# A chunked RWKV-7 recurrence: products of 64 x 64 in quarters of the array in place of products over the whole array

## The chip, the cores and the metric

One core of a Trainium2 chip runs one launch. The metric is the device time of that launch in microseconds, median of three runs; the kernel before has 4324.55 us (4307.94 to 4329.31). All data of the part that is changed is float32.

## The reference, cut to what matters

Two blocks of a network follow each other. The second mixes 1280 tokens (256 of context, 1024 others) with three branches: a state-space branch, an RWKV-7 branch, and a gated linear attention. The change lies in the RWKV branch alone, which has 4 heads of 64 features, is run forward and backward, and is this scan:

```python
def step(S, inp):
    r_t, w_t, k_t, v_t, kk_t, a_t = inp
    sa = -jnp.einsum('nhvk,nhk->nhv', S, kk_t)
    S = S * w_t[:, :, None, :] + sa[..., None] * (kk_t * a_t)[:, :, None, :] + v_t[..., None] * k_t[:, :, None, :]
    return S, jnp.einsum('nhvk,nhk->nhv', S, r_t)
```

Outputs are wanted for the 1024 other tokens only; the context tokens feed the state.

## The kernel before, in words

`mixers` (L1350) runs the three branches. `rwkv_prep` has written, ahead of the loop, the scaled features of each stretch of 128 tokens (`rec`: b, c, p, and for the 1024 tokens q) and the inverses of small triangular blocks (`xd`) to memory. `rwkv_loop` (L1629) does the scan in chunks of 64 tokens (two to a stretch of 128, j = 0, 1), for two heads at a time (h = 0, 1). It has 40 items: 2 pairs of heads (ft) x 2 directions (d) x 10 stretches (g). Per item the steps are:

- `fetch`: loads `rec` and, at times, the inverses `XD`.
- `pairs` (L1671, per head): the masked products of features over tokens, `M`, 128 tokens x 128 tokens per head, of which the blocks off the chunks' diagonal are masked to zero.
- `rights` (L1683): three transposes by TensorE, a product with the values, and two copies by ScalarE: right sides `R`, and `bc`.
- `solve0`, `solve1`, `solve2`: multiply by the block inverse, by the off-diagonal block, and by the inverse again (ScalarE, VectorE, ScalarE copy out); they give `U`.
- `steps` (L1722, per chunk): the map of the state over one chunk, as a 128 x 128 block matrix `gt` of two heads, and what is added, `ze`. Only its diagonal 64 x 64 blocks are written (VectorE adds the identity at L1737, ScalarE scales at L1738); the rest stays zero from six tiles cleared once.
- `queries`, `inside`: the queries carried to the chunk's start, and the part of the output within the chunk.
- `states` (L1767, per chunk): the output from the state (`yp`) and the new state `S`, 128 x 128 with two diagonal blocks. This is the only chain from item to item.

The steps of several items overlap: `seq` (L1794) gives each step a lag in items and an order. `YP` says behind which steps the loop yields; at each yield `mixers` runs a part of the side work, 3 parts an item: `gla` (gated attention; its scores are L1971 on TensorE and L1976, a masked copy, on VectorE) and then `ssd`. Over the first items it also runs `gates`, vector products whose weights are loaded (L167). Within this order a scheduler places each engine's instructions by when it thinks their inputs come. Each engine then runs its list in order.

PSUM has eight banks. In the loop `LPS` gives four to the loop's steps (`mm`), two to side work (`tr`), one to `po` (the state's output) and one to the gates (`gv`):

```python
YP = 7, 12
LPS = dict(mm=4, tr=2, po=1, gv=1)
seq = ((fetch, 0), (rights, 3), (steps, 4, 0), (solve0, 3), (steps, 4, 1), (solve1, 3), (queries, 4),
       (states, 5, 0), (solve2, 3), (inside, 4), (pairs, 2, 0), (states, 5, 1), (pairs, 2, 1))
```

A float32 product is two instructions on TensorE (each with its load of the stationary operand); a transpose is one.

Of the kernel before, what the change touches and what calls it, by code (L numbers as in the profile page):

```python
# [20 lines left out]
P = 128  # L21
# [18 lines left out]
class K:  # L40
# [176 lines left out]
YP = 7, 12  # L217
LPS = dict(mm=4, tr=2, po=1, gv=1)
# [907 lines left out]
def b2_constants():  # L1126
# [3 lines left out]
    same = (s // 64) == (t // 64)  # L1130
    lo, hi = (s % 64) < 32, (t % 64) >= 32
# [8 lines left out]
    put("m_0", np.concatenate([same & lo & hi, same & (s <= t), same & (s < t), same & (s <= t)], 1))  # L1140
    put("m_1", np.concatenate([same & ~lo & ~hi, same & (s >= t), same & (s > t), same & (s >= t)], 1))
# [26 lines left out]
class Mixer:  # L1168
# [460 lines left out]
    def rwkv_loop(self, es):  # L1629
# [12 lines left out]
        mm = [self.const(sp, f"m_{d}").rearrange("p (m a b) -> p m a b", m=2, a=2) for d in range(2)]  # L1642
        NG = 6
# [3 lines left out]
        for t in xds + gts + zes:  # L1647
            nc.gpsimd.memset(t, 0.0)
        n_step, S, n_xd, xd_now = [0], [None], [0], {}

        def fetch(st, it):
            ft, d, g, first = it
            rec = sp.tile([P, 4, P], F32, name="rec", bufs=6)
            w_ = 4 if g >= CT else 3
            k.load(rec[:, :w_], self.rec_d[d][ft][g].rearrange("p (a n) -> p a n", n=P)[:, :w_])
            si = 0 if g < CT else 1 + (g - CT) // 4
            g0, ng = CHUNKS[si][0] // P, CHUNKS[si][1] // P
            if (ft, d, si) not in xd_now:
                xt = xds[n_xd[0] % 3]
                n_xd[0] += 1  # L1660
                src = self.xd[d][ft][si]
                for bb in range(4):
                    o = slice(bb * 32, bb * 32 + 32)
                    for h in range(2):
                        k.load(xt[o, h, :ng, o], src[h * ng:(h + 1) * ng, bb].rearrange("n s t -> s n t"))
                xd_now[ft, d, si] = xt
            st.update(b=rec[:, 0], c=rec[:, 1], p=rec[:, 2], pq=rec[:, 2:2 + w_ - 2],
                      X=xd_now[ft, d, si][:, :, g - g0], V=vtm[:, g, ft * P:(ft + 1) * P]
                      .rearrange("p (h x) -> p h x", x=64))

        def pairs(st, it, h):  # L1671
# [3 lines left out]
            if h == 0:  # L1675
                st["M"] = sp.tile([P, 2, 2, 2, P], F32, name="M", bufs=3)
            f = slice(64 * h, 64 * h + 64)
            pm = k.bank().rearrange("p (m a b) -> p m a b", m=2, a=2)[:, :, :w_]
            for m, src in ((0, st["b"]), (1, st["c"])):
                nc.tensor.matmul(pm[:, m], src[f], st["pq"][f], start=True, stop=True)  # L1680
            nc.vector.tensor_tensor(st["M"][:, h, :, :w_], pm, mm[d][:, :, :w_], op=OP.mult)

        def rights(st, it):  # L1683

            M, V = st["M"], st["V"]
            ps = k.bank()
            nc.tensor.transpose(ps[:, :P], st["p"], k.ident)
            for i, nm in enumerate("bc"):
                nc.tensor.transpose(ps[:, (2 + i) * P:(3 + i) * P], st[nm], k.ident)
            for h in range(2):  # L1690
                nc.tensor.matmul(ps[:, P + h * 64:P + h * 64 + 64], M[:, h, 1, 0], V[:, h], start=True, stop=True)
            R = sp.tile([P, 2, 2, 64], F32, name="R", bufs=2)
            nc.scalar.activation(R, ps[:, :2 * P].rearrange("p (a h x) -> p h a x", h=2, x=64), AF.Copy)
            bc = sp.tile([P, 2, P], F32, name="bc", bufs=2)
            nc.scalar.activation(bc, ps[:, 2 * P:].rearrange("p (a n) -> p a n", n=P), AF.Copy)
            st.update(R=R.rearrange("p h a x -> p h (a x)"), bt=bc[:, 0], ct=bc[:, 1])

        def solve0(st, it):
            U1 = sp.tile([P, 2, P], F32, name="U1", bufs=2)
            ps = k.bank()  # L1700
            for h in range(2):
                nc.tensor.matmul(ps[:, h * P:(h + 1) * P], st["X"][:, h], st["R"][:, h], start=True, stop=True)
            nc.scalar.activation(U1, ps[:, :2 * P].rearrange("p (h x) -> p h x", x=P), AF.Copy)
            st["U1"] = U1

        def solve1(st, it):
            ps = k.bank()
            U1 = st["U1"]
            for h in range(2):
                nc.tensor.matmul(ps[:, h * P:(h + 1) * P], st["M"][:, h, 0, 0], U1[:, h], start=True, stop=True)  # L1710
            nc.vector.scalar_tensor_tensor(U1, ps[:, :2 * P].rearrange("p (h x) -> p h x", x=P), -1.0, st["R"],
                                           op0=OP.mult, op1=OP.add)

        def solve2(st, it):
            U = sp.tile([P, 2, 2, 64], F32, name="U", bufs=2)
            ps = k.bank()
            for h in range(2):
                nc.tensor.matmul(ps[:, h * P:(h + 1) * P], st["X"][:, h], st["U1"][:, h], start=True, stop=True)
            nc.scalar.activation(U, ps[:, :2 * P].rearrange("p (h a x) -> p a h x", a=2, x=64), AF.Copy, scale=-1.0)
            st["U"] = U  # L1720

        def steps(st, it, j):  # L1722

            ft, d, g, first = it
            V, U = st["V"], st["U"]
            ch = slice(64 * j, 64 * j + 64)
            e = self.eend[:, ft, d, 2 * g + j:2 * g + j + 1]
            gt, ze = gts[n_step[0] % NG], zes[n_step[0] % NG]
            n_step[0] += 1
            ps = k.bank()  # L1730
            nc.tensor.matmul(ps[:, :P], U[ch, 0], st["bt"][ch], start=True, stop=True)
            pz = ps[:, P:2 * P].rearrange("p (h x) -> p h x", x=64)
            nc.tensor.matmul(pz, st["bt"][ch], U[ch, 1], start=True, stop=False)
            nc.tensor.matmul(pz, st["ct"][ch], V[ch], start=False, stop=True)
            for h in range(2):
                f = slice(64 * h, 64 * h + 64)
                nc.vector.tensor_tensor(gt[f, f], ps[f, f], k.ident[f, f], op=OP.add)  # L1737
                nc.scalar.activation(ze[f, f], ps[f, P + 64 * h:P + 64 * h + 64], AF.Copy, scale=e[f])  # L1738
            st["step", j] = gt, ze, e

        def queries(st, it):
            if it[2] < CT:
                return
            qt = sp.tile([P, P], F32, name="qt", bufs=2)
            ps = k.bank()
            for h in range(2):
                nc.tensor.matmul(ps[64 * h:64 * h + 64, :P], st["U"][:, 0, h], st["M"][:, h, 0, 1], start=True, stop=True)
            nc.vector.tensor_tensor(qt, ps[:, :P], st["pq"][:, 1], op=OP.add)
            st["qt"] = qt

        def inside(st, it):
# [5 lines left out]
            yc = k.bank()[:, :P].rearrange("p (h x) -> p h x", x=64)  # L1757
            for h in range(2):
                nc.tensor.matmul(yc[:, h], M[:, h, 1, 1], V[:, h], start=True, stop=False)
                nc.tensor.matmul(yc[:, h], M[:, h, 0, 1], U[:, 1, h], start=False, stop=True)  # L1760
            o = Y[:, g - CT, 2 * ft:2 * ft + 2]
            if d == 0:
                nc.scalar.activation(o, yc, AF.Copy)
            else:
                nc.vector.tensor_tensor(o, yc, o, op=OP.add)

        def states(st, it, i):  # L1767
            ft, d, g, first = it
            j = i if d == 0 else 1 - i
            if first and i == 0:  # L1770
                S[0] = sp.tile([P, P], F32, name="S", bufs=3)
                nc.gpsimd.memset(S[0], 0.0)
            ch = slice(64 * j, 64 * j + 64)
            gt, ze, e = st["step", j]
            if g >= CT:
                if i == 0:
                    st["yp"] = k.bank(tag="po")[:, :P].rearrange("p (h x) -> p h x", x=64)
                nc.tensor.matmul(st["yp"][ch], st["qt"][:, ch], S[0].rearrange("p (h x) -> p h x", x=64), start=True,
                                 stop=True)
            ps = k.bank()  # L1780
            nc.tensor.matmul(ps[:, :P], gt, S[0], start=True, stop=True)
            S[0] = sp.tile([P, P], F32, name="S", bufs=3)
            nc.vector.scalar_tensor_tensor(S[0], ps[:, :P], e, ze, op0=OP.mult, op1=OP.add)
            if g >= CT and i == 1:
                o = Y[:, g - CT, 2 * ft:2 * ft + 2]
                nc.vector.tensor_tensor(o, st["yp"], o, op=OP.add)
# [1135 lines left out]
```

## Time and profile before

| | |
|---|---|
| runs | 4324.55 us median (4307.94, 4324.55, 4329.31) |
| profiled execution | 4346.18 us, its span 4344.4 us |
| TensorE busy in the span | 3970.7 us (91%), 23047 products' instructions |
| VectorE | 2888.9 us (66%) |
| ScalarE | 1993.5 us (46%) |
| GpSimd | 1175.7 us (27%) |
| mean granted clock of TensorE | 0.94 |

The clock is a share of 2.4 GHz: 1.00 is 2.4 GHz, 0.50 is 1.2 GHz. Products are pipelined, so a row's duration of one product holds its way through the array; how fast they follow each other is read from the starts of a timeline. A busy share over the whole span is a mean over stages of different kinds; the loop is about an eighth of it.

### The profile page before, as it was taken

The page shows a single profiled execution, that of the slowest core. Times are in us where ns is not written, and L with a number is a line of the kernel's source. Part 1 is how long each engine was busy: PE and PEld are TensorE (multiplying, and loading weights), DVE is VectorE, ACT ScalarE, POOL GpSimd, SP SyncE. Part 2 cuts the span into 40 slices and gives each one's busy share as a digit, 9 for nine tenths or more (in the row PEclk, how much of TensorE's full clock was granted, in tenths as well). Part 3 has the DMA queues.
Part 4 walks back from the last instruction along what each step waited for, and adds up shares of the span by engine and source line. Part 5 has one row for each costly group of instructions (what it writes and reads, how often), then busy time and mean ns, then how long its engine had stood idle before and what let it go on. Part 6 is the DMA issues. An engine that isn't in the chain of part 4 may idle for free. (4 is left out here: it accounts for less than half of the span.)

```text
span 4344.4 us, 63290 instructions
## 1 busy us (share of the span) xinstructions
PE 3970.7 (91%) x23047; PEld 3033.1 (70%) x23048; DVE 2888.9 (66%) x5672; ACT 1993.5 (46%) x4292; POOL 1175.7 (27%) x1211
## 2 busy tenths in 40 slices
PE   6999899999998999999997999999999998999993
PEld 4787566667775666688786788777777666666662
DVE  4673577764745778645765655667778777776774
ACT  4122366653122666423353233433257666666664
POOL 1200133332101333321333531122313232233323
PEclk7999899999998999999997899799999999999996
DMA  5121600123123001344444511215368888889885
GB/s 152 34 66 40 166 13 13 31 81 109 43 63 107 8 13 35 113 120 129 126 124 130 143 35 34 74 42 185 118 210 293 286 247 272 267 261 274 261 264 163
DMA packets 371321, 558.89 MB, mean 129 GB/s; under 512 B 52126, under 2 KB 285056, under 8 KB 346048
## 3 DMA queue, kind: packets, MB, share of 16 engines
q1 hardware_dynamic: 335728, 432.81, 31.2%
q0 software_dynamic: 35280, 122.02, 11.0%
q8 instruction: 182, 2.98, 0.3%
q14 instruction: 131, 1.07, 0.1%
HBM read 438.42 MB, written 116.33 MB: 128 GB/s over the span
## 5 line engine op out<-in xcount | busy, mean ns | idle before, releaser
L98 DVE TENSOR_TENSOR wa_lo<-w_raw,wa_hi 128x512 fp32r<-128x512 f32 x520 | 340.4, 688 | 59.5 <-ACT wa_hi L97 56.7
L97 ACT ACTIVATE wa_hi<-w_raw 128x512 fp32r<-128x512 f32 x520 | 303.5, 625 | 99.3 <-PE mm L109 48.5
L107 PE MATMUL mm<-hh,w_hi 128*128 128x512 f32 (+1 forms) x848 | 320.7, 379 | 4.1 <-ACT h L266 3.3
L108 PE MATMUL mm<-hl,w_hi 128*128 128x512 f32 (+1 forms) x848 | 319.8, 377 | 0.3 <-DVE hl L269 0.3
L109 PE MATMUL mm<-hh,w_lo 128*128 128x512 f32 (+1 forms) x848 | 318.0, 375 | 0.0
L941 ACT ACTIVATE pe<-mm 128x512 f32<-128x512 f32 (+1 forms) x336 | 193.3, 588 | 153.4 <-PE mm L109 124.7
L907 DVE TENSOR_REDUCE mx<-mm 128x1 f32<-128x512 f32 (+1 forms) x400 | 224.3, 587 | 51.6 <-PE mm L906 49.3
L107 PE MATMUL mm<-wa_hi,xh 128*128 128x512 f32 (+3 forms) x632 | 257.6, 408 | 0.5 <-ACT xh L97 0.5
L108 PE MATMUL mm<-wa_lo,xh 128*128 128x512 f32 (+3 forms) x632 | 251.0, 397 | 1.2 <-DVE wa_lo L98 1.2
L109 PE MATMUL mm<-wa_hi,xl 128*128 128x512 f32 (+3 forms) x632 | 250.2, 396 | 0.0
L946 POOL TENSOR_TENSOR pl<-pe,ph 128x512 fp32r<-128x512 f32 x96 | 142.6, 1487 | 333.0 <-ACT ph L945 326.1
L2644 POOL DMA_INDIRECT acc_d<-y,ix x97 | 172.5, 1778 | 202.7 <-DMA acc_d<-y,ix 54.7
L946 DVE TENSOR_TENSOR pl<-pe,ph 128x512 fp32r<-128x512 f32 (+1 forms) x240 | 202.2, 855 | 36.9 <-ACT ph L945 35.8
L610 DVE SCALAR_TENSOR_TENSOR acc<-zc,b_v,acc 128x512 f32<-128x512 f32 (+1 forms) x300 | 199.3, 712 | 1.5
L2600 PE MATMUL mm<-ident,xg 128*128 128x128 f32 (+5 forms) x840 | 121.7, 291 | 85.0 <-DMA xg<-h_d,ix 84.8
L2589 POOL COPY wc<-xg 128x1 f32<-128x1 f32 (+5 forms) x97 | 47.8, 492 | 531.6 <-DMA xg<-h_d,ix 528.4
L107 PEld LDWEIGHTS mm<-hh,w_hi 128*128 128x128 f32 x848 | 162.0, 191 | 40.1 <-issue 7.4
L2600 PEld LDWEIGHTS mm<-ident,xg 128*128 128x128 f32 (+5 forms) x840 | 110.7, 199 | 112.6 <-issue 99.3
L107 PE MATMUL mm<-wb_hi,hidh 128*128 128x512 f32 (+5 forms) x420 | 186.8, 445 | 0.0
L108 PEld LDWEIGHTS mm<-hl,w_hi 128*128 128x128 f32 x848 | 162.1, 191 | 33.8 <-issue 6.5
L97 ACT ACTIVATE w_hi<-w_raw 128x1024 fp32r<-128x1024 f32 x61 | 64.6, 1060 | 259.5 <-PE mm L108 230.6
L109 PEld LDWEIGHTS mm<-hh,w_lo 128*128 128x128 f32 x848 | 162.2, 191 | 28.8 <-issue 1.3
(782 smaller groups left out, 11555.7 us busy)
## 6 DMA issues: line engine op xcount, KB each, us to landing
w_raw<-in_exp_w_dram SPq DMA_DIRECT2D x192, 1024.0 KB
w_raw<-in_w_in_dram SPq DMA_DIRECT2D x69, 512.0 KB
gemv_w<-in_w_mod_dram SPq DMA_DIRECT2D x48, 512.0 KB
gemv_w<-in_ada_w_dram SPq DMA_DIRECT2D x48, 512.0 KB
rec<-rec SPq DMA_DIRECT2D x64, 256.0 KB
wo_raw<-in_w_out_dram SPq DMA_DIRECT2D x20, 512.0 KB
y<-ydram SPq DMA_DIRECT2D x36, 256.0 KB
xt<-in_x_dram SPq DMA_DIRECT2D x16, 512.0 KB
```

Source lines behind the costliest of these rows:

```text
L97: nc.scalar.activation(hi, src, AF.Copy)
L98: eng.tensor_tensor(lo, src, f32(hi), op=OP.subtract)
L107: mm(out, ah, bh, start=start, stop=False)
L108: mm(out, ah, bl, start=False, stop=False)
L109: mm(out, al, bh, start=False, stop=stop)
L610: nc.vector.scalar_tensor_tensor(o, zc[:, ft, p0 + j:p0 + j + c[1]], v["cfw"][:, 2 * j + ft:2 * j + ft + 1], o, op0=OP.mult, op1=OP.add)
L907: nc.vector.tensor_reduce(mx[:, t, c:c + 1], ps[:, :n], axis=AX.X, op=OP.max)
L941: nc.scalar.activation(pe, ps, AF.Exp)
L946: (nc.gpsimd if j % PLP == PLP - 1 else nc.vector).tensor_tensor(pl, pe, f32(ph), op=OP.subtract)
L2589: nc.gpsimd.tensor_copy(st.wc[:n], st.x[:n, D + st.r:D + st.r + 1])
L2600: nc.tensor.transpose(ps[:, j * n:(j + 1) * n], xk[:, 4 * q + j], k.ident[:n, :n])
L2644: nc.gpsimd.indirect_dma_start(out=self.acc_d, out_offset=bass.IndirectOffsetOnAxis(ap=st.ix[:n, 0:1], axis=0), in_=y[:n], in_offset=None, ...
```

## The change

Every product of the loop becomes one of 64 rows (the contracted dimension) by 64 columns, in one of four quarters of the array; the four products of a step, one for each head h and chunk j, go to the four quarters. What a step writes goes to a pair of banks (`pair`), the bank chosen by which half of the rows the product reads. Layouts alternate: where a step reads partitions by heads it writes partitions by chunks, and the other way round. `M` holds only the 64 x 64 diagonal blocks, the state is 128 x 64 (two heads, no zero blocks), the identity is added by a product with the identity matrix in place of VectorE's sum, and the query's carry is part of `steps`. The transposes are plain products with the identity (`turn`). The state is copied out in halves by VectorE and ScalarE. Three pairs serve the loop, one bank side work, one the gates; the chain over items is six deep. Cut to its core:

```diff
+    def pair(self):
+        return self.ps.tile([P, 2, 512], F32, name="m2", tag="m2", bufs=self.bufs["m2"])
-YP = 7, 12
-LPS = dict(mm=4, tr=2, po=1, gv=1)
+YP = 5, 10
+LPS = dict(m2=3, tr=1, gv=1)
...
-        gts = [sp.tile([P, P], F32, name=f"gt{i}") for i in range(NG)]
-        zes = [sp.tile([P, P], F32, name=f"ze{i}") for i in range(NG)]
-        xds = [sp.tile([P, 2, 4, P], F32, name=f"XD{i}") for i in range(3)]
+        xds = [sp.tile([P, 4, 2, 64], F32, name=f"XD{i}") for i in range(3)]
+        half = [slice(0, 64), slice(64, 128)]
+        quarters = [(h, j) for h in range(2) for j in range(2)]
+        mm = nc.tensor.matmul
...
-            rec = sp.tile([P, 4, P], F32, name="rec", bufs=6)
+            rec = sp.tile([P, 4, P], F32, name="rec", bufs=8)
...
+            pm = k.pair()
+            pv = pm[:, :, :256].rearrange("p h (m a t) -> p h m a t", m=2, a=2)
             for m, src in ((0, st["b"]), (1, st["c"])):
-                nc.tensor.matmul(pm[:, m], src[f], st["pq"][f], start=True, stop=True)
-            nc.vector.tensor_tensor(st["M"][:, h, :, :w_], pm, mm[d][:, :, :w_], op=OP.mult)
+                for h, j in quarters:
+                    mm(pv[half[j], h, m, :w_], src[half[h], half[j]], st["pq"][half[h], :, half[j]], start=True, stop=True)
+                nc.vector.tensor_tensor(M.rearrange("p h m a t -> p h (m a t)"), pm[:, :, :256],
+                                        mask[d].unsqueeze(1).to_broadcast([P, 2, 256]), op=OP.mult)
...
+        def turn(st, it):
+            ps = k.pair()
+            for i, nm in enumerate("bc"):
+                for h, j in quarters:
+                    mm(ps[half[j], h, 64 * i:64 * i + 64], st[nm][half[h], half[j]], k.ident[half[h], half[h]], start=True,
+                       stop=True)
+            for j in range(2):
+                for h in range(2):
+                    mm(ps[half[h], h, P + 64 * j:P + 64 * j + 64], st["p"][half[h], half[j]], k.ident[half[h], half[h]],
+                       start=True, stop=True)
...
         def rights(st, it):
+            ps = k.pair()
+            for h, j in quarters:
+                mm(ps[half[h], j, :64], st["M"][half[j], h, 1, 0], st["V"][half[j], h], start=True, stop=True)
+            nc.vector.tensor_copy(st["R"][:, :, 1], ps[:, :, :64])
+
+        def by_x(st):
+            ps = k.pair()
+            for h, j in quarters:
+                mm(ps[half[j], h, :P], st["X"][half[h], j], st["R"][half[h], j].rearrange("p a x -> p (a x)"), start=True,
+                   stop=True)
+            return ps[:, :, :P]
...
+        def steps(st, it):
+            ps = k.pair()
+            for h, j in quarters:
+                mm(ps[half[h], j, :64], U[half[j], h, 0], bc[half[j], h, 0], start=True, stop=True)
...
+            gz = st["gz"] = sp.tile([P, 2, 3, 64], F32, name="gz", bufs=2)
+            nc.scalar.activation(gz[:, :, :w], ps[:, :, :64 * w].rearrange("p j (w x) -> p j w x", x=64), AF.Copy)
...
         def states(st, it, i):
-            nc.tensor.matmul(ps[:, :P], gt, S[0], start=True, stop=True)
-            S[0] = sp.tile([P, P], F32, name="S", bufs=3)
-            nc.vector.scalar_tensor_tensor(S[0], ps[:, :P], e, ze, op0=OP.mult, op1=OP.add)
+            ps = k.pair()
+            for n, (a, b) in enumerate(((k.ident, gz[:, j, 1]), (k.ident, S[0]), (gz[:, j, 0], S[0]))):
+                for h in range(2):
+                    f = half[h]
+                    mm(ps[f, h, :64], a[f, f] if a is k.ident else a[f], b[f], start=n == 0, stop=n == 2)
+            if g >= CT:
+                for n, a in enumerate((st["q"][:, half[j]], gz[:, j, 2])):
+                    for h in range(2):
+                        mm(ps[half[j], h, 64:P], a[half[h]], S[0][half[h]], start=n == 0, stop=n == 1)
+            S[0] = sp.tile([P, 64], F32, name="S", bufs=3)
+            nc.vector.tensor_scalar(S[0][:64], ps[:64, 0, :64], e[:64], None, op0=OP.mult)
+            nc.scalar.activation(S[0][64:], ps[64:, 1, :64], AF.Copy, scale=e[64:])
...
-        seq = ((fetch, 0), (rights, 3), (steps, 4, 0), (solve0, 3), (steps, 4, 1), (solve1, 3), (queries, 4),
-               (states, 5, 0), (solve2, 3), (inside, 4), (pairs, 2, 0), (states, 5, 1), (pairs, 2, 1))
+        seq = ((fetch, 0), (rights, 3), (solve1, 4), (states, 6, 0), (solve0, 3), (pairs, 2), (solve2, 4), (states, 6, 1),
+               (turn, 2), (steps, 5), (inside, 5))
```

The order on TensorE in one steady item of the loop before, from solve1 to pairs (L1710 solve1, L1747 queries, L1778 and L1781 states, L1971 the side work's scores, L1718 solve2, L1759 and L1760 inside, L1680 pairs):

```order
9767 L1710 MATMUL mm<-U_24168,M 128x128 x2
9768 L1747 MATMUL mm<-M,U 64x128 x2
9769 L1778 MATMUL mm<-S,qt 64x128
9770 L1781 MATMUL mm<-S,gt_21629 128x128
9771 L1971 MATMUL mm<-aq,kz_22220 128x128 x4
9772 L1718 MATMUL mm<-U_24168,XD_21642 128x128 x2
9773 L1759 MATMUL mm<-vtm,M 128x64
9774 L1760 MATMUL mm<-U,M 128x64
9775 L1759 MATMUL mm<-vtm,M 128x64
9776 L1760 MATMUL mm<-U,M 128x64
9777 L1680 MATMUL mm<-rec 128x256 x2
9778 L1778 MATMUL mm<-S,qt 64x128
```

And of the changed kernel, from rights to solve2 (L1716 rights, L1733 solve1, L1789 and L1793 states, L1722 the two solves by the inverse, L1686 pairs, L1985 the side work's scores):

```order
9809 L1716 MATMUL m_24725<-vtm,M 64x64 x4
9810 L1733 MATMUL m_24731<-U_24596,M 64x128 x4
9811 L1789 MATMUL m_24737<-gz,ident 64x64
9812 L1985 MATMUL mm<-aq,kz_22224 128x128 x4
9813 L1789 MATMUL m_24737<-gz,ident 64x64
9814 L1789 MATMUL m_24737<-S,ident 64x64 x2
9815 L1789 MATMUL m_24737<-S,gz 64x64 x2
9816 L1793 MATMUL m_24737<-S,rec 64x64 x2
9817 L1793 MATMUL m_24737<-S,gz 64x64 x2
9818 L1722 MATMUL m_24753<-R,XD_21630 64x128 x4
9819 L1686 MATMUL m_24760<-rec 64x128 x8
9820 L1985 MATMUL mm<-aq,kz_22225 128x128 x4
```

The loop's products now come in fours and eights of one shape, and only side work stands between them with another; it comes at three places of an item in place of two.

On VectorE the same piece of an item, before (L1711 solve1's copy, L1737 the map gt, L1783 the state, L1681 the masks, L1966 and L1976 side work):

```order
2563 L1783 SCALAR_TENSOR_TENSOR S<-mm,eend,ze_21636 128x128
2564 L1786 TENSOR_TENSOR Y<-mm,Y 128x128
2565 L1681 TENSOR_TENSOR M<-mm,c_m_21626 128x512
2566 L1976 COPY_PREDICATED AT<-lev,mm 128x512 x2
2567 L1966 TENSOR_TENSOR kz_22216<-ak,kx 32x512
2568 L1737 TENSOR_TENSOR gt_21628<-mm,ident 64x64 x2
2569 L1737 TENSOR_TENSOR gt_21629<-mm,ident 64x64
2570 L1711 SCALAR_TENSOR_TENSOR U_24055<-mm,R 128x256
```

and changed (L1717 rights' copy, L1735 solve1's, L1796 half of the state, L1800 and L1776 the output, L1688 the masks, L1990 side work):

```order
2587 L1990 COPY_PREDICATED AT<-lev,mm 128x512
2588 L1717 COPY R<-m_25312 128x2x64
2589 L1735 TENSOR_TENSOR R<-R,m_25318 128x256
2590 L1990 COPY_PREDICATED AT<-lev,mm 128x512
2591 L1796 TENSOR_SCALAR S<-m_25324,eend 64x64
2592 L1800 TENSOR_TENSOR Y<-m_25324,Y 64x128
2593 L1688 TENSOR_TENSOR M<-m_25347,c_m_21624 128x512
2594 L1990 COPY_PREDICATED AT<-lev,mm 128x512
2595 L1796 TENSOR_SCALAR S<-m_25370,eend 64x64
2596 L1800 TENSOR_TENSOR Y<-m_25370,Y 64x128
```

The four gt and one of two masks are gone, and side work's copies stand one by one between the loop's.

## Rows read from the trace of the kernel before

**Rows 1.** Busy time of each engine by stretch of the loop; columns in the first row.

```profile
core 0: us, PE busy (x) PEld busy (x) DVE busy (x) ACT busy (x) POOL busy (x), PEclk, DMA share, GB/s
2319.00:2409.00 90.00, 67.19 (x390) 46.03 (x394) 43.07 (x97) 34.29 (x56) 36.74 (x29) 0.57 0.51 148
2409.00:2465.00 56.00, 50.11 (x604) 36.62 (x601) 43.26 (x88) 12.32 (x26) 32.23 (x37) 0.95 0.59 172
2465.00:2709.00 244.00, 240.62 (x1804) 201.98 (x1805) 136.75 (x330) 76.56 (x207) 63.61 (x73) 0.99 0.16 45
2709.00:2721.00 12.00, 11.98 (x83) 9.44 (x80) 5.30 (x17) 4.23 (x14) 6.50 (x11) 1.00 0.26 69
2721.00:2769.00 48.00, 47.40 (x175) 35.91 (x175) 24.02 (x55) 21.73 (x48) 4.67 (x22) 0.51 0.28 85
2769.00:2904.00 135.00, 133.04 (x810) 104.04 (x810) 92.17 (x194) 51.78 (x143) 25.11 (x30) 1.00 0.11 34
```

**Rows 2.** Waits of TensorE from 2465 to 2904 us, the two longest totals.

```profile
PE mm L1710 <- ACT U L1703: 2.2, 2, 1.8
PE mm L2159 <- POOL xw L2155: 1.2, 2, 0.9
```

**Rows 3.** Timeline of TensorE over one item: start us, length us, instruction, count.

```profile
2604.42 0.27 PE L1687 MATMUL mm<-ident,rec 128*128 128x128 f32 x1
...
2607.60 0.71 PE L1710 MATMUL mm<-U,M 128*128 128x128 f32 x4
2608.24 0.44 PE L1747 MATMUL mm<-M,U 128*64 128x128 f32 x4
2608.51 0.38 PE L1778 MATMUL mm<-S,qt 128*64 128x128 f32 x2
...
2609.15 1.06 PE L1971 MATMUL mm<-aq,kz 128*128 128x128 f32 x8
2610.04 0.61 PE L1718 MATMUL mm<-U,XD 128*128 128x128 f32 x4
2610.49 0.33 PE L1759 MATMUL mm<-vtm,M 128*128 128x64 f32 x2
...
2614.32 2.05 PE L1971 MATMUL mm<-aq,kz 128*128 128x128 f32 x16
2616.21 0.27 PE L1687 MATMUL mm<-ident,rec 128*128 128x128 f32 x1
```

**Rows 4.** Timeline of TensorE at two places with products in parts of the array.

```profile
449.66 0.64 PE L167 MATMUL mm<-gemv_w,gemv_c 128*32 128x128 f32 x16
...
2010.42 0.38 PE L1546 MATMUL mm<-rec 64*32 64x32 f32 x32
2010.73 0.39 PE L116 MATMUL mm<-b_hh,ws 128*128 128x256 f32 x1
```

**Rows 5.** Groups of VectorE and ScalarE, 2465 to 2709 us: count, busy us, mean ns, idle before.

```profile
L1976 DVE COPY_PREDICATED AT<-lev,mm 128x512 f32<-128x512 uint8 x48 | 35.1, 731 | 16.8 <-PE mm L1971 16.6
L1681 DVE TENSOR_TENSOR M<-mm,c_m 128x512 f32<-128x512 f32 x32 | 22.1, 690 | 18.5 <-PE mm L1680 18.4
L1737 DVE TENSOR_TENSOR gt<-mm,ident 64x64 f32<-64x64 f32 x80 | 17.7, 222 | 26.9 <-PE mm L1734 16.2 <-ACT ze L1738 9.4
L1783 DVE SCALAR_TENSOR_TENSOR S<-mm,eend,ze 128x128 f32<-128x128 f32 x40 | 13.9, 349 | 2.6 <-PE mm L1781 1.3
L1711 DVE SCALAR_TENSOR_TENSOR U<-mm,R 128x256 f32<-128x256 f32 x20 | 8.5, 423 | 9.0 <-PE mm L1710 8.5 <-ACT ak L2017 0.5
...
L1738 ACT ACTIVATE ze<-mm,eend 64x64 f32<-64x64 f32 x80 | 24.7, 309 | 32.4 <-DVE gt L1737 31.7
L1695 ACT ACTIVATE bc<-mm 128x256 f32<-128x256 f32 x20 | 7.6, 378 | 0.0
```

**Rows 6.** Timeline of TensorE, 2708.5 to 2718.4 us: the starts of two items.

```profile
2708.85 0.27 PE L1687 MATMUL mm<-ident,rec 128*128 128x128 f32 x1
...
2718.27 0.33 PE L1687 MATMUL mm<-ident,rec 128*128 128x128 f32 x1
```

More of the change, by code (lines that the diff above doesn't have):

```diff
@@ L1138, in put @@
         out.append(a)
-    put("m_0", np.concatenate([same & lo & hi, same & (s <= t), same & (s < t), same & (s <= t)], 1))
-    put("m_1", np.concatenate([same & ~lo & ~hi, same & (s >= t), same & (s > t), same & (s >= t)], 1))
+    s6, t6 = s % 64, np.arange(64)[None, :]
+    put("m_0", np.concatenate([(s6 < 32) & (t6 >= 32), s6 <= t6, s6 < t6, s6 <= t6], 1))
+    put("m_1", np.concatenate([(s6 >= 32) & (t6 < 32), s6 >= t6, s6 > t6, s6 >= t6], 1))
     b = np.arange(32)[None, :]
@@ L1661, in fetch @@
                 src = self.xd[d][ft][si]
[L1662 to L1665, printed above, removed]
+                for h in range(2):
+                    for bb in range(4):
+                        j, q = divmod(bb, 2)
+                        k.load(xt[h * 64 + q * 32:h * 64 + q * 32 + 32, :ng, j, q * 32:q * 32 + 32],
+                               src[h * ng:(h + 1) * ng, bb].rearrange("n s t -> s n t"))
@@ L1681, in pairs @@
-            nc.vector.tensor_tensor(st["M"][:, h, :, :w_], pm, mm[d][:, :, :w_], op=OP.mult)
-        def rights(st, it):
[L1685 to L1696, printed above, removed]
@@ L1698, in solve0 @@
-        def solve0(st, it):
[L1699 to L1704, printed above, removed]
-        def solve1(st, it):
[L1707 to L1712, printed above, removed]
@@ L1714, in solve2 @@
-        def solve2(st, it):
[L1715 to L1749, printed above, removed]
+                for h, j in quarters:
+                    mm(pv[half[j], h, m, :w_], src[half[h], half[j]], st["pq"][half[h], :, half[j]], start=True, stop=True)
@@ new lines, in steps @@
+        def steps(st, it):
+            M, V, U, bc = (st[n] for n in ("M", "V", "U", "bc"))
+            w = 3 if it[2] >= CT else 2
+            ps = k.pair()
+            for h, j in quarters:
+                mm(ps[half[h], j, :64], U[half[j], h, 0], bc[half[j], h, 0], start=True, stop=True)
+            for h, j in quarters:
+                mm(ps[half[h], j, 64:P], bc[half[j], h, 0], U[half[j], h, 1], start=True, stop=False)
+            for h, j in quarters:
+                mm(ps[half[h], j, 64:P], bc[half[j], h, 1], V[half[j], h], start=False, stop=True)
+            if w == 3:
+                for h, j in quarters:
+                    mm(ps[half[h], j, P:P + 64], U[half[j], h, 0], M[half[j], h, 0, 1], start=True, stop=True)
+            gz = st["gz"] = sp.tile([P, 2, 3, 64], F32, name="gz", bufs=2)
+            nc.scalar.activation(gz[:, :, :w], ps[:, :, :64 * w].rearrange("p j (w x) -> p j w x", x=64), AF.Copy)
@@ L1756, in inside @@
             M, V, U = st["M"], st["V"], st["U"]
-            yc = k.bank()[:, :P].rearrange("p (h x) -> p h x", x=64)
+            ps = k.pair()
             for h in range(2):
[L1759 to L1765, printed above, removed]
+                o = slice(64 * h, 64 * h + 64)
+                for j in range(2):
+                    mm(ps[half[j], j, o], M[half[j], h, 1, 1], V[half[j], h], start=True, stop=False)
+                for j in range(2):
+                    mm(ps[half[j], j, o], M[half[j], h, 0, 1], U[half[j], h, 1], start=False, stop=True)
+            for j in range(2):
+                o, y = Y[half[j], g - CT, 2 * ft:2 * ft + 2], ps[half[j], j, :P].rearrange("p (h x) -> p h x", x=64)
+                if d == 0:
+                    nc.scalar.activation(o, y, AF.Copy)
+                else:
+                    nc.vector.tensor_tensor(o, y, o, op=OP.add)
         def states(st, it, i):
```

57 lines of the change are left out of this document (32 added, 25 removed).

## Prediction

> **What bounds the kernel now.** I read the span in stretches first. The RWKV loop runs from about 2319 to 2904 us, and TensorE is busy in nearly all of it: 240.62 of 244 us in the middle stretch, 133.04 of 135 us in the last [rows 1]. VectorE has 136.75 and ScalarE 76.56 of those 244 us. The waits say the same: over 440 us the longest total that TensorE waited for one line is 2.2 us [rows 2]. So here the time is TensorE's own. Only the first 90 us differ: 67.19 us busy, clock 0.57, the DMA engines at 0.51 of their time [rows 1].
>
> One steady item by the timeline: from one L1687 to the next is 2616.21 - 2604.42 = 11.79 us. The side work in it (gated attention, L1971) takes 2610.04 - 2609.15 = 0.89 and 2616.21 - 2614.32 = 1.89 us, 2.78 together; RWKV has the other 9.01 us [rows 3]. L1711 runs once per item, 20 times in the 244 us of the middle stretch [rows 5], so an item takes 12.2 us there. The loop has 40 items (2 x 2 x 10); I put six ahead of that stretch and 14 behind it.
>
> **The change part by part.** *Products.* A product is two instructions of TensorE (L1718: two products, x4 [rows 3]). Before, an item has 59 instructions, nearly each filling the array for about 0.11 us: L1718's four take 2610.49 - 2610.04 = 0.45 us [rows 3]. Now it has 80 products, 160 instructions, each in one quarter. What counts is the fullest quarter. Of 128 moved columns it has 4 instructions in pairs and 6 in the three solves, 10. Of 64 columns it has 8 in turn, 2 in rights, 8 in steps, 8 in inside (two quarters do all of it) and 10 in each call of states, 46.
>
> Price: in L167 four column quarters have 16 instructions of 128 columns, four each, in 0.64 us, and one product's instruction lasts 0.27 us (the first of rows 3), so (0.64 - 0.27) / 3 = 0.12 us from one to the next in a quarter [rows 3, 4]. That is the price of the ten. No row has 64 x 64. Bounds: L1546, 64 x 32 with 32 columns, puts 32 instructions over four quarters in 2010.73 - 2010.42 = 0.31 us, 0.04 us each in its quarter [rows 4]; the other end is 0.12. I take 0.06, half the column price, as half as many columns are moved and loaded. RWKV: 10 x 0.12 + 46 x 0.06 = 4.0 us (bounds 3.0 and 6.7).
>
> The row of L1546 also shows instructions starting on average 0.31 / 32 = 0.01 us apart [rows 4], so issue is no limit. The Trainium skill, TensorE: Matmul & The Clock Gate, under "Wait — 56ns, not 53.3ns?", has start to start never below about 25 ns; the row contradicts that for quarters, and by the rule an item would have at least 160 x 0.025 = 4.0 us, the same as my sum.
>
> *Changes of shape.* L1710's four instructions, between products of other shapes, take 2608.24 - 2607.60 = 0.64 us against L1718's 0.45: 0.19 us for two changes, 0.095 each [rows 3]. The item before has eleven, about 1.0 us of its 9.01. The order after has six in a steady item, all at side work: 0.6 us.
>
> *Transposes.* Three of one instruction become twelve plain products; they are in the 8 of turn.
>
> *VectorE, ScalarE.* VectorE now has 136.75 / 20 = 6.8 us an item. Gone: one masked M of two (0.69), four gt (4 x 0.22), the query sum (bounded by 0.35); two S shrink from 0.35 towards 0.22; new: a copy of R and a second Y (at most 0.35 each) [rows 1, 5]. That leaves 5.5 to 5.8. On ScalarE four ze of 0.31 go; half of S twice, R in two pieces and gz come, about 0.3 to 0.5 us each by L1738 and L1695 [rows 5]; its 76.56 / 20 = 3.8 us stay near 4. Neither passes 7.4 us, but the cover gets thin.
>
> *Banks.* A step takes a pair of banks and three pairs go round, where four single banks served; side work has one bank for its results where it had two. A step's pair is wanted again three steps later, about 3 x 0.4 us. A result is copied out in 0.38 to 0.69 us (L1695, L1681), behind whatever stands ahead on that engine, a 0.73 us AT among it [rows 5]. Bounds of the new wait: nothing, or one such hold-up of 0.7 us at four of the ten steps, 2.9 us an item. I take 1.4, the middle, as the order puts side work between the steps that share an engine.
>
> *Queues, depth.* SP issues the same loads in the same order, two smaller; POOL loses the clears of twelve tiles, and is busy 63.61 of 244 us [rows 1]: nothing, hidden by TensorE. The chain over items is six deep, not five: one more short round, 2 to 4 us, taken in the start below.
>
> *Sum.* A steady item: 4.0 + 0.6 + 2.78 + 1.4 = 8.8 us in place of 11.8, so 3.0 saved. Middle: 20 x 3.0 = 60. Last part: 14 items, RWKV as before but side work that follows other engines, so the wait is longer: 2.5 each, 35. Start: six items, 18 us at 3.0; the clock of 0.57 makes each worth more, but TensorE waits in a quarter of that time anyway [rows 1] and the deeper chain costs: 15. Together 110 us. The profiled run has 4346.18 us, span 4344.4; 4346 - 110 = 4236. That run is 21.6 us above the median 4324.55, so the forecast in runs is **4215 us**.
>
> **The rivals.** *The copies out become the bound.* For it: VectorE and ScalarE keep almost all they had while TensorE's share falls, and there are three pairs. Against: 5.8 of 8.8 us is not full. With the full 2.9 us an item saves 1.5: 20 x 1.5 + 14 x 1 + 6 = 50, 4275 us. The Trainium skill, TensorEngine Tiling (Array Packing), "PSUM Bottleneck", warns of just this: after fourfold products the copies out of PSUM may bound.
>
> *No new wait.* The order is good enough, TensorE stays full: 7.4 us an item, 4.4 saved; 88 + 14 x 4 + 16 = 160, 4165 us.
>
> *The quarters don't run four at a time.* Column parts side by side are in the rows (L167, L1546, and L1747, whose four take 0.27 us, not 0.45 [rows 3, 4]); two row halves at once are in none. If they take turns, RWKV is 2 x 4.0 + 0.6 = 8.6, an item 8.6 + 2.78 = 11.4 and 0.6 of wait: 12.0 against 12.2 at most. No change, 4325 us.
>
> *The clock falls, slower.* TensorE's granted clock went to 0.51 for 48 us from 2721 on, though it was busy for 47.40 of them [rows 1]; the levels are 2.4 and 1.2 GHz. Just before, an item took 2718.27 - 2708.85 = 9.4 us [rows 6], hardly more than RWKV's own 9.0: its products had run almost alone. Instructions there came every 48 / 175 = 0.27 us against 135 / 810 = 0.17. Quarter products that wait between steps could keep the chip at 1.2 GHz through most of the loop. Then 7.4 x 1.8 = 13.3 us an item (between the 1.65 of these rows and 2), waits hidden: 1.5 x 20 = 30 lost in the middle and, with side work slowed too, about 40 behind: 4395 us. It decides where more than about half of the loop has the low clock. Against: side work stays as dense as it was, and at 2465 to 2709 the clock was 0.99.
>
> **How the numbers follow.** My sum 0.50, copies as bound 0.20, no wait 0.13, halves in turn 0.08, low clock 0.09. A measurement of this kernel can tell about 0.5% (22 us) from no change. Faster than 4303: the first and third case and most of the second, 0.80; within: the rest of the second and most of the fourth, 0.09; slower: 0.11. The range takes in 4165 with the cheaper product price and 4275 with some more wait: 4150 to 4300; it leaves out the halves and the low clock, 0.17.
>
> **What would show it.** Right: the loop some 475 us long instead of 585; a steady item near 8.8 us; the four instructions of a solve step starting within a few hundredths of a us; RWKV's lines near 4 us an item; clock near 1.0 in the middle. The wait term is right if TensorE's waits for VectorE and ScalarE are about 1.4 us an item. Wrong: a solve step whose lower half starts only when the upper is through, a middle stretch at clock 0.5, or items of over 10 us with TensorE idle behind copies.

## The result

The changed kernel takes 4274.49 us (median of four runs, 4267.59 to 4276.94), the kernel before beside it 4325.9 us. The ratio is 0.988, 95% interval 0.985 to 0.991: 51 us faster, where 110 were forecast. The time fell, by luck, on that of the rival in which the copies out become the bound (4275 us): the runs below lay most of the loss to another bank than the pairs that this rival spoke of.

To compare the loop I cut it at points of equal work: the first product of RWKV, the fourth and the eighth output of gated attention (og, L1997 before, L2011 after), the last product of RWKV. Stage I has the start and the first half of gated attention, stage II exactly twelve items of its second half, stage III the state space work. Windows of the kernel before, at these points (columns as in [rows 1]):

```profile
2327.89:2570.05 242.16, 221.03 (x1846) 168.84 (x1846) 135.29 (x303) 80.91 (x174) 96.34 (x86) 0.84 0.39 112
2570.05:2712.05 142.00, 139.94 (x969) 118.38 (x969) 80.23 (x194) 44.00 (x120) 32.22 (x37) 0.99 0.12 32
2712.05:2914.38 202.33, 199.75 (x1105) 154.37 (x1105) 126.33 (x279) 80.21 (x213) 35.22 (x62) 0.88 0.18 56
```

And of the changed kernel:

```profile
2327.51:2553.61 226.10, 175.20 (x2978) 128.44 (x2978) 117.48 (x255) 82.36 (x179) 94.46 (x85) 0.83 0.45 127
2553.61:2674.32 120.71, 104.25 (x2102) 91.19 (x2102) 63.98 (x148) 43.99 (x118) 32.58 (x38) 0.92 0.13 35
2674.32:2840.92 166.60, 141.15 (x2696) 103.92 (x2689) 108.91 (x231) 85.21 (x226) 30.87 (x64) 0.91 0.23 69
```

The loop went from 586.5 to 513.4 us. In stage II an item went from 142.00 / 12 = 11.83 to 120.71 / 12 = 10.06 us; 8.8 were forecast. TensorE, busy for all but 2 of 142 us before, is now idle for 120.71 - 104.25 = 16.5 us there, and its granted clock is 0.92 in place of 0.99. VectorE has 63.98 / 12 = 5.3 us an item and ScalarE 3.7, a little less than forecast.

The quarters do what was forecast of them. The timeline of TensorE in the changed kernel, parts of one item (start, length, instruction, count):

```profile
2619.24 0.34 PE L1716 MATMUL m<-vtm,M 64*64 64x64 f32 x8
2619.41 0.40 PE L1733 MATMUL m<-U,M 64*64 64x128 f32 x8
2619.63 0.27 PE L1789 MATMUL m<-gz,ident 64*64 64x64 f32 x2
...
2624.91 0.29 PE L1749 MATMUL m<-U,bc 64*64 64x64 f32 x8
2625.02 0.29 PE L1751 MATMUL m<-vtm,bc 64*64 64x64 f32 x8
2625.14 0.29 PE L1754 MATMUL m<-M,U 64*64 64x64 f32 x8
...
2627.29 0.33 PE L1716 MATMUL m<-vtm,M 64*64 64x64 f32 x5
```

L1749's eight instructions, two in each quarter, take 2625.02 - 2624.91 = 0.11 us, 0.06 each in their quarter; L1733's eight of 128 columns take 2619.63 - 2619.41 = 0.22 us, 0.11 each. Both are the prices of the sum (0.06 and 0.12), and this item, without a long wait, took 2627.29 - 2619.24 = 8.05 us.

What takes its place is in the list of TensorE's waits of the changed kernel from 2465 to 2841 us (us in total, times, longest), to be held against [rows 2]:

```profile
PE mm L1998 <- DVE og L2011: 9.6, 6, 2.5
PE m L1768 <- DVE Y L1800: 5.9, 8, 3.0
PE m L1768 <- ACT R L1710: 5.7, 5, 1.7
PE mm L1985 <- DVE AT L1990: 4.2, 16, 0.3
PE m L1733 <- ACT gz L1756: 3.2, 6, 1.1
```

The longest row is no wait of RWKV (L1768's two, 11.6 us together, are waits for copies out, of the kind that the prediction priced). L1998 is the first product of an output of gated attention, which needs the one side bank that the output before it still holds. The timeline of one such hold-up, all engines:

```profile
2650.03 0.65 PE L2002 MATMUL mm<-Sl,qd 128*128 128x256 f32 x2
2650.72 0.38 ACT L2006 ACTIVATE sq<-mm 128x256 f32<-128x256 f32 x1 [0.84 <-PE mm L2002]
2651.24 0.41 DVE L2007 TENSOR_REDUCE st<-sq 128x4 f32<-128x256 f32 x1
2651.74 0.19 POOL L89 TENSOR_SCALAR st<-st 128x4 f32<-128x4 f32 x1 [13.07 <-DVE st L2007]
...
2653.11 0.61 POOL L2010 TENSOR_TENSOR og<-og,st 128x256 f32<-128x256 f32 x1
2653.75 0.42 DVE L2011 TENSOR_TENSOR og<-mm,og 128x256 f32<-128x256 f32 x1 [1.60 <-POOL og L2010]
...
2654.32 1.19 PE L1998 MATMUL mm<-Sl,qd 128*128 128x256 f32 x2 [1.85 <-DVE og L2011]
```

From the last product of an output (2650.03 + 0.65) to the end of og (2653.75 + 0.42) the bank is held for 3.5 us, by a chain over ScalarE, VectorE and GpSimd. L1998 of the next output starts 0.15 us behind it.

### The profile page after: what moved, and what is told of

The parts are those of the page before. It is cut to its first block, busy times and chain, and to the rows that moved or that the text cites. A ratio compares the mean times of both kernels' runs of the same rounds, so it can differ in the third digit from the quotient of the medians.

```text
span 4265.8 us, 70842 instructions
## 1 busy us (share of the span) xinstructions
PE 3821.9 (90%) x26895; PEld 2912.7 (68%) x26896; DVE 2832.1 (66%) x5528; ACT 1996.6 (47%) x4308; POOL 1158.9 (27%) x1199
## 5 line engine op out<-in xcount | busy, mean ns | idle before, releaser
L113 PEld LDWEIGHTS mm<-hh,w_lo 128*128 128x128 f32 x848 | 162.3, 191 | 28.6 <-issue 1.3
```

Of the source, the lines that this page charges most:

```text
L113: mm(out, al, bh, start=False, stop=stop)
```

## The experiments

Theory A is that the one side bank (`tr`) is the loss, with the clock that falls in its waits. Theory B: the three pairs of RWKV and their copies. Theory C: the clock falls by itself under quarter products. Theory D: the sum was set against an execution of the kernel before that happened to be long. Ratios are against the kernel before, run beside each group.

**The kernel before, a second trace; no edit.**

> The kernel before, unchanged, for a second trace of it. Theory D (the sum was set against a run that was itself drawn long: its 4346 us lie 20 above the median, part of it a half-clock stretch at 2721 to 2769 us): this run comes at 4320 to 4330 us with no such stretch or a shorter one, and the loop takes 555 to 565 us. Against it: about 4345 us again in the profiled execution, the stretch of half clock in the same place and the loop at 575 us, so that a profiled run is always that much longer than the others.

It took 4325.45 us. Its windows at the same points:

```profile
2324.36:2572.73 248.37, 223.18 (x1846) 170.50 (x1846) 139.05 (x302) 80.82 (x174) 95.93 (x86) 0.83 0.39 109
2572.73:2716.22 143.49, 141.44 (x969) 119.87 (x969) 80.20 (x193) 44.03 (x120) 32.16 (x37) 0.98 0.12 32
2716.22:2904.57 188.35, 183.00 (x1105) 141.57 (x1105) 125.82 (x279) 80.07 (x213) 35.15 (x62) 0.98 0.19 59
```

Stage III takes 188.35 us at a clock of 0.98, where the first trace had 202.33 at 0.88: most of the 48 us at half clock [rows 1] belonged to that one execution, and were worth 14 us. D holds for stage III. Stage I is 6 us longer in this trace, though, so that the loop is only 6 us shorter as a whole: 580.21 us by these cuts, not 555 to 565. Against this trace the changed kernel's stages save 22, 23 and 22 us.

**The changed kernel again; no edit.**

> The changed kernel, unchanged, timed beside the three experiments. Expected 4267 to 4277 us and a ratio of 0.988 to the kernel before. Theory A (one side bank): the long items sit again at the outputs of gated attention (L1998), each with TensorE idle until og L2011. Theory C (the granted clock falls by itself under quarter products): the falls lie at other places in this trace, and items without any wait are slow where the clock is low.

4276.53 us, ratio 0.987 (0.984 to 0.991), which is 59 us under the kernel before in this group. Stages of 230.6, 117.5 and 166.0 us, waits of 8.4 us at L1998 for og. Item by item its long places are those of the first trace. At the end of stage II one item with outputs takes 20.4 us here, against 20.6, by the starts of VectorE's copy of R (L1717). Of the four stretches at half clock in stage II two come again, both at these outputs; C's picture of falls in other places does not show.

**Two banks for the outputs alone.**

```diff
-                po = k.bank(tag="tr")[:, :256]
+                po = k.bank(tag=("tr", "gv")[c % 2])[:, :256]
```

> The changed kernel; only the eight outputs of gated attention take their bank alternately from tr and from gv, which has been idle since the gates ended at about 2475 us. Theory A (the one side bank, at the outputs above all): the 9.6 us that TensorE waits at L1998 for og L2011 go, the clock falls that follow them as well, and the run is 10 to 25 us shorter than the changed kernel (4250 to 4264). Theory B (the three pairs and their copies out hold TensorE): the waits come back at the next pair, under 5 us gained. Theory C (the clock by itself): under 5 us, falls in the clock as before.

4262.15 us, ratio 0.984 (0.981 to 0.987), 14 us under the changed kernel. No wait of L1998 for og is left, and stage II falls to 110.27 us at a clock of 0.98:

```profile
2544.13:2654.40 110.27, 95.71 (x2110) 83.56 (x2110) 64.41 (x151) 43.65 (x118) 31.40 (x37) 0.98 0.14 39
```

One line, run at eight outputs, holds a quarter of the 59 us that were missing (110 forecast, 51 measured): A. But TensorE's idle time in stage II fell by 1.9 us only (16.46 to 14.56), though 6.6 us of waits for og are gone: L1686 and L1722 now wait 4.3 us there for copies of R, 0.2 before, and so much of B is right. Its busy time fell by 8.5 us (104.25 to 95.71; by 5.3 against the second trace of the changed kernel). Most of what one bank costs there is thus not waiting, but products that run at half clock around the waits.

**Two banks for all side work, first try.** This run had a switch in the function that gives out banks, which should have closed when the gates end; its condition was never true, as `n` and `S2` are both 1.5.

```diff
+        if tag == "tr" and self.both:
+            self.both = 3 - self.both
+            tag = ("tr", "gv")[self.both - 1]
...
-                        run(gates, int(due + 1e-6))
+                        if run(gates, int(due + 1e-6)) and not k.both and n != S2:
+                            k.both = 1
```

> The changed kernel; once the gates have ended, all side work of the loop takes tr and gv in turn, so that it has two banks as in the kernel before. Theory A: besides the outputs the waits of the scores for AT (4.2 us at L1985) and those of the state space part for one bank go: 20 to 35 us shorter than the changed kernel (4240 to 4255). Theory B: no more than 8 us, with the waits of L1722, L1733, L1768 for copies of R, gz and Y as long as they were or longer. Theory C: under 5 us.

4279.05 us, ratio 0.988 (0.985 to 0.991). It says nothing of the theories: it is the changed kernel a second time, and shows how well that repeats.

**Two banks for all side work.**

```diff
-                        if run(gates, int(due + 1e-6)) and not k.both and n != S2:
+                        if run(gates, int(due + 1e-6)) and not k.both and "tr" in LPS and k.bufs["tr"] == 1:
```

> The changed kernel, with all side work of the loop taking tr and gv in turn from the end of the gates on; the run before it (side2) had the same aim, but its switch never closed, so that it was the changed kernel once more. Theory A (one side bank): 15 to 35 us shorter than the changed kernel, at least as good as the run with two banks at the outputs alone (4262), as the transposes of the state space part (L2152, 3.5 us of waits for the copy bt) gain as well. Theory B (pairs and their copies): no better than 4262, the waits for AT, R, gz and Y as before.

4243.72 us, ratio 0.980 (0.978 to 0.982): 33 us under the changed kernel (4276.53, from another group), 90 under the kernel before, and the best version of this study. Its windows at the same points:

```profile
2324.60:2541.41 216.81, 167.76 (x2968) 124.83 (x2968) 120.95 (x254) 82.49 (x179) 97.14 (x85) 0.85 0.47 132
2541.41:2648.79 107.38, 95.33 (x2112) 84.29 (x2112) 62.97 (x151) 43.49 (x118) 32.72 (x37) 0.97 0.16 40
2648.79:2809.44 160.65, 133.92 (x2695) 103.00 (x2695) 110.10 (x231) 86.91 (x234) 34.03 (x64) 0.94 0.25 72
```

Stage II takes 107.38 / 12 = 8.95 us an item, against 8.8 in the forecast; the clock is back at 0.97 with nothing done about it. The loop is 28.6 us shorter than in the changed kernel, 484.8 in place of 513.4 us. Only 5 of these us are idle time of TensorE (92.8 to 87.8), the other 24 are busy time (420.6 to 397.0) with the same products. By a count in the two traces two things differ in it: TensorE is busy at half clock for 66 us of the loop, against 99, and it changes between RWKV's lines and side work's 53 times in stage II, against 71. So the second bank gives a shorter wait, a higher clock and another order all at once, and this run does not part the three. The next output no longer waits (timeline of all engines, L2003 and L2007 the first and last product, L2016 og):

```profile
2632.80 0.65 PE L2007 MATMUL mm<-Sl,qd 128*128 128x256 f32 x2
2633.29 0.59 PE L2003 MATMUL mm<-Sl,qd 128*128 128x256 f32 x2
...
2636.43 0.42 DVE L2016 TENSOR_TENSOR og<-mm,og 128x256 f32<-128x256 f32 x1 [2.10 <-POOL og L2015]
```

**Two pairs, three side banks; then two pairs, four.**

```diff
-LPS = dict(m2=3, tr=1, gv=1)
+LPS = dict(m2=2, tr=3, gv=1)
```

> The changed kernel with two pairs of banks in the ring instead of three, and three side banks instead of one. Theory A (the side bank is the loss, three pairs are enough): near the two-bank runs, 4255 to 4270. Theory B (the wait for a pair that is being copied out bounds): a step now waits for the copy of the step but one before it, some 0.4 to 0.7 us at several of the ten steps of an item, 40 items: 4300 to 4400.

The second takes the same banks, and sends side work round all four (three and gv) once the gates have ended.

> The changed kernel with two pairs of banks and the side work going round four banks (three and gv) once the gates have ended. Theory A (side banks are what is short, two pairs nearly suffice): 4240 to 4262, no slower than two pairs with three side banks. Theory B (pairs): stays at 4262 or above, while three pairs with two side banks take 4244, and in the stretch between the last outputs of the two halves of gated attention TensorE waits more than the 12.8 us it waits there with three pairs and two side banks.

4262.27 us, ratio 0.983 (0.981 to 0.985), and 4262.46, ratio 0.983 (0.981 to 0.985). A pair taken away, which B has as a loss of some 25 us or more, is a gain of 14 as long as the side work gets banks for it; a fourth side bank adds nothing. Three pairs with two side banks are still 19 us better (4243.72). Stage II of these two, in this order:

```profile
2549.23:2660.47 111.24, 101.93 (x2106) 81.70 (x2106) 63.80 (x150) 44.11 (x119) 31.26 (x37) 1.00 0.14 38
2557.01:2668.26 111.25, 101.95 (x2106) 81.71 (x2106) 63.87 (x151) 44.18 (x119) 31.33 (x37) 1.00 0.14 38
```

TensorE waits for 9.3 us, less than the 12.05 us with three pairs and two side banks, so B's wait is not there. It is busy longer in these 12 items, though: 101.95 us at a clock of 1.00 against 95.33 at 0.97. The order of the work differs: in stage II it goes from RWKV's lines to side work's or back 118 times, against 53, by a count of the instructions in the two traces. If nothing else differs, a change costs at least (101.95 - 95.33) / 65 = 0.10 us; this is an estimate from one pair of runs.

**Both halves of the state on VectorE.**

```diff
-            nc.scalar.activation(S[0][64:], ps[64:, 1, :64], AF.Copy, scale=e[64:])
+            nc.vector.tensor_scalar(S[0][64:], ps[64:, 1, :64], e[64:], None, op0=OP.mult)
```

> The changed kernel, with both halves of the new state on VectorE (the lower half was on ScalarE). In the profile ScalarE's half waits for VectorE's (20.8 us over 29 times behind L1796 from 2553 us on), and VectorE's Y for ScalarE's half (14.4 us, 24 times), though neither needs the other's numbers; TensorE's waits for Y (L1800) come to some 9 us. Theory B (this handshake is a part of the 1.46 us that TensorE waits per item): the waits for Y halve at least and the run is 5 to 12 us shorter. Rival: VectorE gets 0.27 us of work 80 times, 22 us, and where it is full (the convolutions of the state space part, 2684 to 2694) the state comes no earlier: within 4 us of the changed kernel, or up to 6 slower.

4287.85 us, ratio 0.990 (0.986 to 0.993). The median lies 11 us above the changed kernel's 4276.53, more than the 6 that the rival allowed, but the runs scatter from 4266 to 4317 and the two intervals overlap. The stages of the loop take 224.7, 120.9 and 166.7 us, as they did; of the 26 us that its profiled execution is longer than the changed kernel's, 25 lie behind the loop, where the clock is 0.66 in the first 100 us. In the loop TensorE did not depend on the handshake: the wait of L1768 for Y even rose, from 5.9 to 10.2 us. So B's gain is not there; the rival's picture fits the loop, its bound on the time was missed.

**The kernel before with one side bank.**

```diff
-LPS = dict(mm=4, tr=2, po=1, gv=1)
+LPS = dict(mm=5, tr=1, po=1, gv=1)
```

> The kernel before with one side bank in place of two (the bank goes to the RWKV ring, five in place of four). Theory A1 (one bank is a loss by itself): the outputs of gated attention wait for og as in the changed kernel, two items of some 20 us in place of 14, and with the scores' waits the run is 12 to 25 us longer than the kernel before. Theory A2 (one bank costs only where TensorE has too little other work to lie between): an item has 8.5 us of RWKV products there, so most of the chain is covered: 0 to 8 us longer.

4425.19 us, ratio 1.022 (1.019 to 1.024), 92 us longer: far over both expectations. The windows of the three stages and of the 100 us behind the loop:

```profile
2325.97:2586.57 260.60, 238.45 (x1848) 174.62 (x1848) 132.81 (x306) 81.37 (x177) 94.36 (x84) 0.81 0.37 104
2586.57:2731.83 145.26, 142.98 (x968) 118.66 (x969) 78.03 (x191) 43.34 (x117) 32.84 (x38) 1.00 0.12 31
2731.83:2937.34 205.51, 199.28 (x1079) 150.78 (x1078) 123.34 (x276) 77.64 (x204) 31.97 (x63) 0.88 0.16 47
2937.34:3037.34 100.00, 94.59 (x270) 64.36 (x270) 46.89 (x81) 31.24 (x102) 25.60 (x34) 0.54 0.30 86
```

Behind the loop the second trace of the kernel before has:

```profile
2904.57:3004.57 100.00, 92.77 (x479) 68.03 (x478) 78.92 (x127) 45.85 (x142) 31.80 (x48) 0.98 0.52 171
```

In stage II, which has half of the outputs, one bank costs 145.26 - 143.49 = 2 us, where the second bank is worth 13 to the changed kernel (120.71 to 107.38): that fits A2, by which the old kernel's 8.5 us of RWKV an item cover the chain. The rest lies elsewhere, against the second trace: 12 us in stage I, 17 in stage III (3 against the first trace, whose clock was 0.88 there too), and 54 from the end of the loop to the end of the run, where the clock is 0.54 in the first 100 us and not 0.98. The edit changes no product of that stretch. All five runs of this kernel are this long (4412 to 4432 us), so it is no accident of one execution; what held the clock down there stays open, and with it most of the 92 us.

**Three side banks in the kernel before, the control.** The same switch, there over its two side banks and gv.

> Control: the kernel before, where all side work goes round three banks (its two and gv) once the gates have ended. Theory A with a cover (the old kernel's 8.5 us of RWKV products an item hide the side work's chains, the quarter products cannot): within 10 us of the kernel before. Rival: a third bank is worth as much there, so that the 33 us gained by the second bank in the changed kernel are no part of the change: 15 us or more shorter.

4336.81 us, ratio 1.000 (0.999 to 1.002), and stage II takes 142.00 us to the hundredth, as in the first trace. The bank that is worth 33 us in the changed kernel is worth nothing in the old one. Together with the run before it, this makes the loss in stage II one of the change: it took away the second bank and the cover at once. For the rest of the run it is not shown, as the old kernel with one bank lost much there too.

**Products that nobody reads, in the waits of the outputs.**

```diff
                 nc.tensor.matmul(po, qd[1][:, t], Sl[1][:, c], start=False, stop=True)
+                fill = k.bank(tag="gv")
+                for _ in range(2):
+                    nc.tensor.matmul(fill, qd[1][:, t], kx[:, NCTX:NCTX + 512], start=True, stop=True)
```

> The changed kernel with one bank, and after each of the eight outputs of gated attention two products of 512 columns more, on the free bank gv, that nobody reads: TensorE has something to do while it waits for og. Theory C' (a good part of the loss at the outputs is the granted clock that falls with the waits: 19.5 us of TensorE's busy time at half clock between the last outputs of the two halves, half of it lost): the clock stays near 1.0 in that stretch and, though some 14 us of products are added, the run is 0 to 10 us shorter than the changed kernel. Theory A alone (the waits themselves are the loss): the clock falls no less or it does not matter, and the run is 0 to 12 us longer.

4273.89 us, ratio 0.987 (0.984 to 0.989): 3 us under the changed kernel run in another group, which is inside the scatter. Stage II:

```profile
2548.50:2668.77 120.27, 105.93 (x2136) 89.25 (x2136) 64.34 (x149) 44.37 (x119) 32.68 (x38) 0.97 0.13 36
```

The clock went from 0.92 to 0.97, and the stage is as long as it was. The filling products are themselves work over the whole array, so this run alone could not tell waits from quarter products; together with the run with two banks for the outputs, whose clock is 0.98 with quarter products and nothing added, it lays the half clock there to the waits. As an estimate, what it cost is about what the filling costs, some 7 us in stage II (the two products of an output take 1.9 us there). A second bank gives back both.

## Why the prediction was wrong

**Which step failed.** It is the paragraph on banks, and with it the term 2.78 of the sum, which has side work stay on TensorE as it was. The paragraph named both facts, three pairs for RWKV and one bank for side work where there were two, and priced only the first: a new wait of 1.4 us, from single copies out of a pair of 0.38 to 0.73 us. The side bank got no price of its own. It is not held for one copy but for a chain over three engines, 3.5 us for an output of gated attention, and side work has nothing else to go to. With a second side bank 33 of the missing 59 us come back (4276.53 to 4243.72); with a pair fewer and two side banks more 14 do. The rows to see it by were there before: L1997's chain could have been read at its four places of each half, and the cover that hid it, 8.5 us of RWKV an item, is what the sum itself took away.

The Trainium skill, TensorEngine Tiling (Array Packing), "Gotcha 1: PSUM Pressure", says that row tiles raise the demand for PSUM, since different row tiles write to different banks. The runs agree: each step takes a pair of banks, and it was the work outside the loop's products that went short, by the 33 us above. The sentence of the same page that the prediction cited, on copies out that may become the bound, is not borne out in stage II: with a pair fewer TensorE waited less there, 9.3 against 12.05 us.

**Term by term.** Each instruction of TensorE is counted here from the end of the one before it. Over the whole loop, against the second trace of before, RWKV's lines take 365.1 us before and 210.3 after: 154.8 saved, where the prices of a steady item give 40 x (9.01 - 4.6) = 176. Side work takes 182.8 us before and 210.3 after: 27.5 more, where the sum had no change. Idle time goes from 32.6 to 92.8 us: 60.2 more, where 40 x 1.4 = 56 were taken. That is 154.8 - 27.5 - 60.2 = 67.1 us, to the rounding what the loop gained. So the wait has about the size that the sum gave it. What the sum had wrong is TensorE's busy time: side work, which it took as unchanged, and a saving of RWKV taken from one item that was long. With two side banks side work is down to 195.5 us.

In stage II RWKV's lines take 8.54 us an item before and 4.65 after: 4.6 were forecast for products and changes of shape, the sizing that looked least certain. Before, 9.01 were taken from one item, 0.5 too many. Side work takes 3.15 us before and 4.06 after, where 2.78 were taken for both. TensorE is busy at half clock for 20 us of the stage; if half of that is lost, it is 10 us, 0.8 an item, in RWKV's and side work's products together, for which the sum had nothing. TensorE waits for 1.4 us, the very size forecast, but half of it is for something else: of the 16.5 us, 6.6 are for og and 2.1 for AT, both on the side bank. The changed kernel's waits in stage II:

```profile
PE mm L1998 <- DVE og L2011: 5.1, 3, 2.5
PE mm L1985 <- DVE AT L1990: 2.1, 8, 0.3
PE mm L1985 <- DVE og L2011: 1.5, 1, 1.5
```

**By stage.** Forecast were 15 + 8 x 3.0 = 39 us in stage I, 36 in II, 35 in III. The changed kernel, against the second trace of before, has 22, 23 and 22; with two side banks 32, 36 and 28. So with two side banks II comes out to the us, and what is left is 7 us at either end. Their causes are read from the traces, no run tests them. In I TensorE's idle time doubles, from 25.2 to 50.9 us: it waits for things that no product shortens, 8.5 us for a load of rec (9.4 before) and 7.3 for GpSimd's tm (2.1 before) among them. In III VectorE is full for a stretch: in the run with two banks for the outputs it is busy for 10.00 of 10 us from 2684 to 2694, with the convolutions, while TensorE's clock is 0.50. Outside of the loop the changed kernel's trace is 9 us longer than the second one of before, 3 ahead of it and 6 behind; the loop's 67 us are thus 58 of the profiled executions (4325.45 to 4267.59).

**The rivals.** That the halves take turns is excluded by L1733. That the clock falls by itself over half of the loop is excluded too: 0.83, 0.92 and 0.91 in the three stages, against 0.84, 0.99 and 0.88, and 0.97 in stage II as soon as the waits are gone or filled. *The copies out* gave the right time by luck: its wait of 2.9 us an item was not there (1.5 were), and the bank was the wrong one. The profiled run, 21.6 us over the median, was taken as long everywhere; stage III alone was 14 us longer in it than in the second trace, so that a part of what that stage seemed to offer belonged to that execution.

## What to carry to other kernels

When products get shorter, list every buffer whose holder was hidden behind them, and price each by how long its longest chain holds it, not by one copy; work that shares TensorE but not the edit is the first to go short, and its share of the busy time does not stay as it was: the waits bring the clock down for it too. Where a change takes a buffer and the cover of that buffer at the same time, look for one that lies idle in that stretch: here a bank that the gates had left, for 33 us. Check the terms taken as unchanged as well as the new ones. Set the sum against more than one trace of the kernel before, or at least keep a stretch with an odd clock out of it.

## What the runs showed of the chip that I had not expected

Quarter products start 0.11 / 8 = 0.014 us apart, near the 0.01 of L1546. A change between them and full-array products may cost 0.10 us or more, by the estimate from the runs with two pairs, near the 0.095 of the prediction. A stretch can keep TensorE busy and still not get the full clock: 94.59 of 100 us at 0.54 in the old kernel with one side bank, with 270 instructions, where the kernel before had 92.77 at 0.98 with 479. Such stretches lay behind the loop in two traces and in stage III in others, also of one and the same kernel (202 against 188 us); what goes with them is 14 to 54 us, more than most edits here. What decides it stayed open.
